# Interleaving the 32x32 products that join the halves of the chunk inverses

## The chip, the cores and the metric

The kernel runs on one core of one Trainium2 chip. Times are microseconds (us) of device time of that core; a kernel's time is the median of its timed runs. The engines are TensorE (PE; its weight loads are PEld), VectorE (DVE), ScalarE (ACT), GpSimd (POOL) and SyncE (SP), which here issues most DMAs.

## What is computed

Two layers of a diffusion trunk over 256 latent and 256 context tokens, width 2048, in float32. Layer 0 is attention; layer 1 is a bidirectional chunked gated DeltaNet with 32 value heads over 16 key heads, chunks of 64 tokens. The change lies in layer 1, in the triangular solve of each chunk:

```python
def gated_delta_chunked(q, k, v, g, beta, state0):
    ...
    kb = kf * bf[..., None]
    lmat = jnp.where(strict, jnp.einsum('bhncd,bhnsd->bhncs', kb, kf) * decay, 0.0)
    rhs = jnp.concatenate([vf * bf[..., None], kb * jnp.exp(gf)[..., None]], axis=-1)
    sol = lax.linalg.triangular_solve(lmat + jnp.eye(CHUNK, dtype=F32), rhs, left_side=True, lower=True)
    u, w = sol[..., :dv], sol[..., dv:]
    ...

def deltanet_layer(x, ctx, c, c_ctx, ...):
    ...
    o_cf, s_cf = gated_delta_chunked(qc, kc, vc, gc[0], bc[0], zero)
    o_xf, _ = gated_delta_chunked(qx, kx, vx, gx[0], bx[0], s_cf)
    o_cb, s_cb = gated_delta_chunked(flip_t(qc), flip_t(kc), flip_t(vc), flip_t(gc[1]), flip_t(bc[1]), zero)
    o_xb, _ = gated_delta_chunked(flip_t(qx), flip_t(kx), flip_t(vx), flip_t(gx[1]), flip_t(bx[1]), s_cb)
    x = x + gt[:, None] * deltanet_out(o_xf + flip_t(o_xb), zx, o_norm, w_out)
```

## The kernel before

Dense products take a weight tile of 128x1024 that SP loads (`raw`, four buffers), ScalarE rounds to `whi` (L77, three buffers) and VectorE subtracts to give the rest `wlo` (L78, three buffers). Each 128x128 block is then used in three matmuls, L90 to L92, over 512 or 256 tokens into a tile `mm` of PSUM. So every weight tile passes through SP, ScalarE, VectorE and TensorE in that order.

Layer 1 first works on keys, queries and decays of 16 heads: `head(kh)` (L672) runs the dense products, the convolution's taps on VectorE (L561), silu on ScalarE (L572, L575), transposes `ptk` (L679), squares (L682) and norms (L701 on GpSimd, L703), decays `pd` (L711 to L716) in PSUM tiles of the tag `xu`, and products `kk` (L727), and stores its results. From two heads `inverse(sg)` (L743) makes the 32 chunk inverses (two heads, two directions, eight chunks), 64x64 each. The two 32x32 diagonal blocks of all of them are inverted at once on VectorE, with 31 steps of two instructions (L768, L770); X is then scaled (L772) and transposed into `U` both ways (L775, L776).

The block between the two halves is what the change touches. For a direction d and a chunk h of a pair, `left(d, h)` (L782) makes 16 products of 32x32 into `px`, which ScalarE evicts, negated, to `Xs` (L789); `right(d, h, Xs)` (L792) makes 16 more into `pu`, which ScalarE copies into `U` (L799). `px` and `pu` are tiles of one bank of PSUM, of the tag `xu` with two buffers. `quad(b, h)` (L588) is the 32 partitions from 64 b + 32 h on; `tile_position` names the 32 rows and 32 columns of TensorE's array that a product uses. In `left` these are rows 32 h and columns 64 + 32 h; in `right`, rows 64 + 32 h, and columns 32 h for d = 0 and 64 + 32 h for d = 1. All 16 products of one call use the same place. The four `left` calls run one ahead of the four `right` calls (L801 to L809), then SP stores `U` (L811). `U`, `X` and `L` have one buffer each. A product in float32 appears in the trace as two matmul records, each with its weight load.

The order is set by generators. The loop at L884 to L893 has 42 rounds, six for one of the inverses 0 to 6; a round takes seven steps of `inverse` (to the next `yield`), in some rounds a step of the gate units `zunits` at the fourth, and then a step of `heads` (`woven`, L832). The joining falls into the sixth round. Inverse 7 runs by itself, with the last gate units and the first values filled in after every fourth step (L897). Then the scans over the chunks begin, with the value heads' dense products between them. The instruction order on each engine is fixed when the program is built, from the order written and from estimated durations.

Of the kernel before, what the change touches and what calls it, by code (L numbers as in the profile page):

```python
# [26 lines left out]
def trunk_kernel(ctx: ExitStack, tc: tile.TileContext, g):  # L27
# [40 lines left out]
    # ---------------------------------------------------------------- helpers  # L68
# [26 lines left out]
    def sliced(wsrc, units, k0, n, xh, xl, pst, first, last):  # L95
        # n contraction tiles of two units
        m = 128 * n
        raw = wp.tile([128, 1024], F32, name="raw", tag="raw", bufs=4)
        for e in range(2):
            nc.sync.dma_start(raw[:, m * e:m * e + m], wsrc[units[e]][:, 128 * k0:128 * k0 + m])  # L100
        w = split(raw, 2 * m)
        for e in range(2):
            dense(pst[e], [w], m * e, n, xh, xl, k0=k0, first=first, last=last)
# [3 lines left out]
    def adaln(l, ps, pm, tp, order, bufs=3, after=None):  # L107
        # a step for every two weight tiles
        wm, bmod, gain = ((g["ab_wm"], ab_bmod, ab_gain), (g["dn_wm"], dn_bmod, dn_gain))[l]
        for f0, n in order:  # L110
            # n blocks of 128 outputs from f0 on
# [35 lines left out]
    def adaln_lanes(l, ps, pm, tp, chunks, after=None):  # L147
        # the sums over the contraction tiles on the vector engine, those over the partitions at the end
# [36 lines left out]
    def rstd_bcast(squares, nb, dim, ps, tag, tp, sq_tag="sq"):  # L185
        # squares: for every block of tokens the tiles that add up to its squares, summed over the feature tiles
# [18 lines left out]
    def add_squares(acc, srcs, first, tp, n=T, sq_tag="sq", last=False):  # L205
        # the last squares stay apart
        sq = acc if first else tp.tile([128, T], F32, name="sq", tag=sq_tag)
        m = n // len(srcs)
        for i, x in enumerate(srcs):
            A.activation(sq[:, i * m:(i + 1) * m], x, AF.Square)  # L210
        if not first and not last:
            V.tensor_tensor(acc[:, :n], acc[:, :n], sq[:, :n], op=ALU.add)
        return sq
# [22 lines left out]
    # ================================================================ layer 0  # L236
# [6 lines left out]
    with tc.tile_pool(name="s0", bufs=2) as tp, tc.tile_pool(name="s0p", bufs=1, space=PSUM) as ps:  # L243
# [6 lines left out]
        # squares, four feature tiles at a time  # L250
# [51 lines left out]
    with tc.tile_pool(name="ab", bufs=2, reuse_waits="tile") as tp, \  # L302
# [29 lines left out]
        def parts(src, name, n=T, scale=1.0, pool=None, bufs=1):  # L332
            # float32 as the sum of two float32r
# [16 lines left out]
        def attend(qT, kT, vT, h, bias=None, rope=None):  # L350
            # v to token-major
# [58 lines left out]
        # latent ranks and the shared rope key  # L410
# [98 lines left out]
    # ================================================================ layer 1  # L509
    # Tokens of a sequence go in two tiles of two chunks, (0, 3) and (1, 2); inside a tile the order is  # L510
    # (half of the chunk, chunk of the pair, token), so that a 32-partition quadrant is 2 * half + chunk,
    # while the keys are worked on, and (chunk of the pair, token) in the scans.
# [54 lines left out]
    def tile_act(dst, src, func, halves):  # L567
        # to tile order, as (half, chunk, token) or (chunk, token)
# [9 lines left out]
    def by_pair(dst, src):  # L578
        # columns from (half, chunk, token) to (chunk, half, token)
        A.copy(dst.rearrange("p s (h b i) -> p s b h i", h=2, b=2), src.rearrange("p s (b h i) -> p s b h i", b=2, h=2))  # L580

    def by_chunk(dst, src):
        # rows from (half, chunk, token) to (chunk, token)
# [22 lines left out]
    def project(u, p):  # L606
        # output unit to the residual, back from tile order
# [5 lines left out]
    # the scans take over the room of the keys' tiles tag by tag, so that they begin as it is left  # L613
    with tc.tile_pool(name="dn", bufs=2, reuse_waits="tile") as tp, \
            tc.tile_pool(name="dnps", bufs=2, space=PSUM, reuse_waits="tile") as ps:
        # write strength and decay of all heads
# [3 lines left out]
        # of the keys: squared norms inverted, and norms, as the rows lie here and in the scans; of the queries, what  # L620
        # stands for the norm's epsilon once they are not normalized
# [35 lines left out]
        for d in range(2):  # L657
# [3 lines left out]
            # scan arrangement a: chunk h of a pair runs in direction (a + h) % 2  # L661
# [10 lines left out]
        def head(kh):  # L672
# [31 lines left out]
            # the decays [row, column]: forwards for the transposed system, backwards for the system  # L704
            # itself and, within the sequence, transposed
# [27 lines left out]
            for d in range(2):  # L733
                # of a 32-block only what lies on its side of the diagonal is read
# [8 lines left out]
        def inverse(sg):  # L743
            # (norm^2 / beta + L)^-1 of two heads, their keys not normalized, L the system forwards and its transpose backwards: of the
            # 32-blocks on the vector engine, with the unit on the partition
            NTu = NTs[sg].rearrange("p a k s h i -> p (a k s h) i")
            # as the blocks come and transposed
# [31 lines left out]
            # the block between the two halves of a chunk  # L779
            lo, hi = slice(0, 32), slice(32, 64)  # L780

            def left(d, h):  # L782
                r1, r2 = quad(0, h), quad(1, h)
                px = ps.tile([128, 16, 32], F32, name="px", tag="xu")
                for u in range(16):
                    PE.matmul(px[r2, u], NTu[r1, 16 * d + u, hi], U[r1, 1, 16 * d + u, lo], start=True, stop=True,
                              tile_position=(r1.start, r2.start))
                Xs = tp.tile([128, 16, 32], F32, name="Xs", tag="Xs")
                A.mul(Xs[r2], px[r2], -1.0)  # L789
                return Xs  # L790

            def right(d, h, Xs):  # L792
                r2 = quad(1, h)
                out, off = (quad(0, h), hi) if d == 0 else (r2, lo)
                pu = ps.tile([128, 16, 32], F32, name="pu", tag="xu")
                for u in range(16):
                    ab = Xs[r2, u], U[r2, 0, 16 * d + u, hi]
                    PE.matmul(pu[out, u], ab[d], ab[1 - d], start=True, stop=True, tile_position=(r2.start, out.start))  # L798
                A.copy(U[out, d, 16 * d:16 * d + 16, off], pu[out])  # L799

            cur = None  # L801
            for d in range(2):
                for h in range(2):
                    nxt = d, h, left(d, h)
                    if cur:
                        right(*cur)
                        yield
                    cur = nxt
            right(*cur)  # L809
# [12 lines left out]
        def mix(main, filler, n):  # L822
            # one step of the filler after every n of the main work
# [8 lines left out]
        def woven():  # L832
            # the heads one after the other, each with its products begun while the one before it ends
# [71 lines left out]
        def cut(t, i, shape):  # L905
            # piece i of a tile, in a shape
# [11 lines left out]
        # block-diagonal operands: the zeros stay, the blocks come from memory  # L918
# [14 lines left out]
        # of keys and values, the parts that the state's products take  # L933
# [6 lines left out]
        def blocks(dst, src):  # L940
            # [128, 2 (direction), 4, 64] in memory to [128, 2 (arrangement), 4, 128]
# [25 lines left out]
        def step(o, n):  # L967
            # one chunk in both directions, in four parts
# [68 lines left out]
        def finish(o):  # L1037
            # norm and gate of a head, in four parts
# [26 lines left out]
        # of the output products, units below NE take the heads below 12 early  # L1065
        NE = 8
        # weight tiles in the order of their use
# [23 lines left out]
        def tile_mm(p, j, k0, xh, xl, sl, first, last):  # L1091
            # the eight contraction tiles of weight tile j, one at a time
# [12 lines left out]
        def value_unit(q):  # L1105
            # q: unit number after those of head 0; its first step is 2 * q - 2
# [57 lines left out]
        for st in range(-2, 64 + LAG):  # L1164
# [27 lines left out]
            # what follows the products of the unit before  # L1192
# [77 lines left out]
def _layout(inputs):  # L1270
# [5 lines left out]
    def fm(a):  # [tok, feat] -> [128, feat/128, tok]  # L1276
        return np.ascontiguousarray(a.T.reshape(-1, 128, a.shape[0]).transpose(1, 0, 2))

    def units(w, kt=None):  # [K, C] -> [C/128, 128, K/128 * 128]
# [3 lines left out]
    def vec(v):  # [F] -> [128, F/128]  # L1283
        return v.reshape(-1, 128).T
# [24 lines left out]
    # neighbourhood bias, padded outside the window  # L1309
# [10 lines left out]
    # constants of the shapes alone  # L1320
# [10 lines left out]
    # gated delta layer  # L1331
# [45 lines left out]
```

## Time and profile before

| | |
|---|---|
| time, median of 3 runs | 2585.1 us (2583.42 to 2586.82) |
| profiled execution: span from first to last instruction | 2580.0 us |
| mean granted TensorE clock of that execution | 0.985 |
| TensorE, VectorE, ScalarE, GpSimd busy, share of the span | 97%, 72%, 44%, 10% |
| matmul instructions | 16586 |

The page gives one execution. A device time of that execution apart from its span is not given; the median of the three runs lies 5.1 us above the span. Busy shares are averages over stages; a matmul's end is modelled, so a busy TensorE is not TensorE at its peak, and its real pace is the distance between starts. "Idle before" and the arrow behind it say how long an engine stood and what ended that.

### The profile page before, as it was taken

The numbers are of one execution on the slowest core, as the hardware profiler recorded it, in microseconds if no ns is written. First come the engines' busy times: TensorE is split into PE (matmuls) and PEld (weight loads), VectorE is DVE, ScalarE is ACT, GpSimd is POOL, SyncE is SP. The second block draws the span as 40 slices with busy tenths as digits, with TensorE's granted clock in tenths as the row PEclk, the third lists the DMA queues.
The fourth block names the chain that finished last, engine by engine and source line by source line (L and its number), as shares of the span: only waits on it lengthen the run. The fifth ranks groups of instructions, "written<-read, shape, count | busy, mean of one in ns | idle before, by whom it ended". The sixth has DMA issues, their size and how long they took to land.

```text
span 2580.0 us, 43446 instructions
## 1 busy us (share of the span) xinstructions
PE 2499.2 (97%) x16586; PEld 2039.0 (79%) x16586; DVE 1852.2 (72%) x3543; ACT 1146.6 (44%) x2484; POOL 267.4 (10%) x261
## 2 busy tenths in 40 slices
PE   6999999999999999989999999999999999999998
PEld 4657888888767788768888889897777777777898
DVE  4544788773455687758999999987677777777754
ACT  4223323232333422377656655643444445445353
POOL 0000000000000000133212222310000000003000
PEclk9999999999999999999999999999999999999999
DMA  8872655532343376644454544563333433335454
GB/s 258 289 247 90 201 172 167 175 114 96 117 153 100 120 230 221 212 139 157 142 156 152 160 138 150 159 213 100 88 99 115 119 99 106 113 91 174 153 188 140
DMA packets 201810, 394.30 MB, mean 153 GB/s; under 512 B 68225, under 2 KB 109697, under 8 KB 201473
## 3 DMA queue, kind: packets, MB, share of 16 engines
q1 hardware_dynamic: 200448, 389.98, 47.9%
q8 instruction: 131, 2.15, 0.4%
q10 hardware_dynamic: 1152, 1.54, 0.2%
q14 instruction: 79, 0.64, 0.1%
HBM read 356.28 MB, written 35.13 MB: 152 GB/s over the span
## 4 chain that ended last, share of the span: by engine, by line
PE 79%; DVE 9%; issue 6%; DMA 3%; ACT 2%; SPq 0%; POOL 0%; DVEq 0%; POOLq 0%; ACTq 0%
PE mm L90 19%; PE mm L91 18%; PE mm L92 18%; PE pks L982 3%; PE pmod L127 3%; DVE wlo L78 2%; PE sp L348 2%; PE ptr L994 2%; DVE X L770 1%; DVE outer L768 1%; PE po L348 1%; PE pu L798 1%; DVE acc L561 1%; PE ptr L1027 1%; PE psu L1013 1%
## 5 line engine op out<-in xcount | busy, mean ns | idle before, releaser
L90 PE MATMUL mm<-hh,whi 128*128 128x512 f32 (+1 forms) x2784 | 988.5, 355 | 3.7 <-ACT t L636 2.2
L92 PE MATMUL mm<-hh,wlo 128*128 128x512 f32 (+1 forms) x2784 | 962.2, 346 | 8.7 <-DVE wlo L78 7.5
L91 PE MATMUL mm<-hl,whi 128*128 128x512 f32 (+1 forms) x2784 | 963.2, 346 | 0.0
L77 ACT CAST whi<-raw 128x1024 fp32r<-128x1024 f32 (+2 forms) x346 | 338.3, 979 | 668.4 <-PE mm L91 515.6
L90 PEld LDWEIGHTS mm<-hh,whi 128*128 128x128 f32 x2784 | 535.7, 192 | 113.8 <-issue 32.6
L92 PEld LDWEIGHTS mm<-hh,wlo 128*128 128x128 f32 x2784 | 535.4, 192 | 73.1 <-DVE wlo L78 9.4
L91 PEld LDWEIGHTS mm<-hl,whi 128*128 128x128 f32 x2784 | 536.0, 193 | 62.2 <-issue 8.4
L78 DVE TENSOR_TENSOR wlo<-raw,whi 128x1024 fp32r<-128x1024 f32 (+2 forms) x346 | 402.7, 1166 | 212.9 <-ACT whi L77 206.1
L163 DVE SCALAR_TENSOR_TENSOR lacc<-mraw,cond,lacc 128x512 f32<-128x512 f32 x300 | 208.8, 749 | 0.0
L561 DVE SCALAR_TENSOR_TENSOR acc<-cin,taps,acc 128x508 f32<-128x508 f32 (+3 forms) x256 | 196.1, 767 | 6.7 <-ACT acc L552 4.3
L1004 DVE SCALAR_TENSOR_TENSOR vl<-ptr,egm,vh 128x128 fp32r<-128x128 f32 x224 | 64.6, 346 | 98.3 <-ACT rf L1001 39.4
L711 POOL TENSOR_TENSOR rhs<-ghl,incl 128x512 fp32r<-128x512 f32 (+1 forms) x96 | 108.4, 1139 | 133.4 <-PE pd L713 114.2
L127 PE MATMUL pmod<-mraw,cond 128*32 128x512 f32 (+2 forms) x640 | 94.3, 501 | 23.2 <-DMA mraw<-ab_wm 18.6
L768 DVE SCALAR_TENSOR_TENSOR outer<-L,bv,X 128x31 f32<-128x31 f32 (+15 forms) x248 | 112.4, 453 | 4.7
L1088 DVE TENSOR_TENSOR wlo<-raw,whi 128x1024 fp32r<-128x1024 f32 x84 | 102.6, 1222 | 14.4 <-ACT whi L1080 13.8
L194 POOL TENSOR_TENSOR rs<-ms,half 128x4 f32<-128x4 f32 (+1 forms) x5 | 4.7, 947 | 985.1 <-DVE ms L192 985.1
L770 DVE TENSOR_TENSOR X<-X,outer 128x31 f32<-128x31 f32 (+15 forms) x248 | 101.7, 410 | 4.6
L575 ACT ACTIVATE ac<-acc 128x128 f32<-128x128 f32 x160 | 37.4, 300 | 146.0 <-DVE acc L561 146.0
L90 PE MATMUL mm<-gh,whi 128*128 128x512 f32 x256 | 99.9, 392 | 1.7 <-DVE x1B L493 1.7
L91 PE MATMUL mm<-gl,whi 128*128 128x512 f32 x256 | 99.9, 390 | 0.2 <-DVE gl L481 0.2
L92 PE MATMUL mm<-gh,wlo 128*128 128x512 f32 x256 | 99.7, 390 | 0.0
L998 ACT ACTIVATE vh<-ptr,egm 128x128 fp32r<-128x128 f32 x224 | 71.0, 373 | 56.6 <-PE ptr L994 54.6
(289 smaller groups left out, 3629.2 us busy)
## 6 DMA issues: line engine op xcount, KB each, us to landing
raw<-dn_w SPq DMA_DIRECT2D x194, 512.0 KB, 4.0
mraw<-dn_wm SPq DMA_DIRECT2D x96, 512.0 KB, 4.7
mraw<-ab_wm SPq DMA_DIRECT2D x88, 512.0 KB, 5.4
raw<-ab_w SPq DMA_DIRECT2D x66, 512.0 KB, 3.8
raw<-dn_wo SPq DMA_DIRECT2D x64, 512.0 KB, 3.7
raw<-ab_wo SPq DMA_DIRECT2D x32, 512.0 KB, 4.6
raw<-ab_w SPq DMA_DIRECT2D x32, 256.0 KB, 3.6
spt<-sp SPq DMA_DIRECT2D x64, 128.0 KB, 2.8
```

The lines of the kernel that those rows point to most:

```text
L77: A.copy(hi[:, :m], raw[:, :m])
L78: V.tensor_tensor(lo[:, :m], raw[:, :m], hi[:, :m].bitcast(F32), op=ALU.subtract)
L90: PE.matmul(ps, wh[:, c], xh[:, k0 + k, sl], start=first and k == 0, stop=False)
L91: PE.matmul(ps, wh[:, c], xl[:, k0 + k, sl], start=False, stop=False)
L92: end = PE.matmul(ps, wl[:, c], xh[:, k0 + k, sl], start=False, stop=last and k == kt - 1)
L127: PE.matmul(pmod[32 * q:32 * q + 32, :m], cond[:, 4 * kg + q, :], raw[c // 1024][:, half + c % 1024:half + c % 1024 + m], start=kg == 0, s ...
L163: V.scalar_tensor_tensor(acc[:, s], raw[:, q], cond[:, k, s:s + 1], acc[:, s], op0=ALU.mult, op1=ALU.add)
L561: V.scalar_tensor_tensor(o3[:, :, i0:i1], p3[:, :, i0 + d:i1 + d], taps[:, ch, t:t + 1], o3[:, :, i0:i1], op0=ALU.mult, op1=ALU.add)
L711: P.tensor_tensor(rhs, ghl[i].bitcast(F32)[:, d, kh * 8:kh * 8 + 2 * n].unsqueeze(2).broadcast_to(sh), incl[:, c].unsqueeze(1).broadcast_t ...
L768: V.scalar_tensor_tensor(o, L[:, rows, k:k + 1].broadcast_to([128, n, m]), bv[:, k:k + 1], X[:, k:k + 1, cols].broadcast_to([128, n, m]), ...
L770: V.tensor_tensor(X[:, rows, cols], X[:, rows, cols], o, op=ALU.subtract)
L1088: V.tensor_tensor(w, raws[j], h.bitcast(F32), op=ALU.subtract)
```

## The change

`left` now takes a direction and makes the products of both chunks, in turn, into one `px` tile; one eviction of 64 partitions follows. The products of `right` of both directions and both chunks run in one loop, four places of the array in turn, into two `pu` tiles; two copies of 64 partitions follow. The `yield`s lie after each `left` and after the copies, three as before. The arithmetic is the same. Comments are also taken out of the file; those lines of the diff are left out here.

```diff
-            def left(d, h):
-                r1, r2 = quad(0, h), quad(1, h)
+            def left(d):
                 px = ps.tile([128, 16, 32], F32, name="px", tag="xu")
                 for u in range(16):
-                    PE.matmul(px[r2, u], NTu[r1, 16 * d + u, hi], U[r1, 1, 16 * d + u, lo], start=True, stop=True,
-                              tile_position=(r1.start, r2.start))
+                    for h in range(2):
+                        r1, r2 = quad(0, h), quad(1, h)
+                        PE.matmul(px[r2, u], NTu[r1, 16 * d + u, hi], U[r1, 1, 16 * d + u, lo], start=True, stop=True,
+                                  tile_position=(r1.start, r2.start))
                 Xs = tp.tile([128, 16, 32], F32, name="Xs", tag="Xs")
-                A.mul(Xs[r2], px[r2], -1.0)
+                A.mul(Xs[64:128], px[64:128], -1.0)
                 return Xs
 
-            def right(d, h, Xs):
-                r2 = quad(1, h)
-                out, off = (quad(0, h), hi) if d == 0 else (r2, lo)
-                pu = ps.tile([128, 16, 32], F32, name="pu", tag="xu")
-                for u in range(16):
-                    ab = Xs[r2, u], U[r2, 0, 16 * d + u, hi]
-                    PE.matmul(pu[out, u], ab[d], ab[1 - d], start=True, stop=True, tile_position=(r2.start, out.start))
-                A.copy(U[out, d, 16 * d:16 * d + 16, off], pu[out])
-
-            cur = None
+            Xs = []
             for d in range(2):
-                for h in range(2):
-                    nxt = d, h, left(d, h)
-                    if cur:
-                        right(*cur)
-                        yield
-                    cur = nxt
-            right(*cur)
+                Xs.append(left(d))
+                yield
+            pu = [ps.tile([128, 16, 32], F32, name="pu", tag="xu") for _ in range(2)]
+            for u in range(16):
+                for d in range(2):
+                    for h in range(2):
+                        r2 = quad(1, h)
+                        out = quad(0, h) if d == 0 else r2
+                        ab = Xs[d][r2, u], U[r2, 0, 16 * d + u, hi]
+                        PE.matmul(pu[d][out, u], ab[d], ab[1 - d], start=True, stop=True,
+                                  tile_position=(r2.start, out.start))
+            for d in range(2):
+                out, off = (slice(0, 64), hi) if d == 0 else (slice(64, 128), lo)
+                A.copy(U[out, d, 16 * d:16 * d + 16, off], pu[d][out])
+            yield
             for d in range(2):
                 by_chunk(spu[sg][:, d], U[:, d, 16 * d:16 * d + 16])
```

## Rows read from the trace of the kernel before

**Rows 1.** The page: busy time of each engine (us, share of the span, instructions), and the chain of work that ended last, by engine.
```profile
PE 2499.2 (97%) x16586; PEld 2039.0 (79%) x16586; DVE 1852.2 (72%) x3543; ACT 1146.6 (44%) x2484; POOL 267.4 (10%) x261
...
PE 79%; DVE 9%; issue 6%; DMA 3%; ACT 2%; SPq 0%; POOL 0%; DVEq 0%; POOLq 0%; ACTq 0%
```

**Rows 2.** Busy time by stretches of the layer-1 stage, in turn the 24 us from the first `px` product of an inverse on and the stretch up to the next one. Columns: stretch, its length, then busy us of PE, PEld, DVE, ACT and POOL with their instructions, mean granted TensorE clock, share of the DMA engines, GB/s.
```profile
1259.00:1283.00 24.00, 23.82 (x401) 22.51 (x401) 21.66 (x44) 14.69 (x32) 4.67 (x8) 1.00 0.52 146
1283.00:1337.00 54.00, 50.89 (x330) 45.87 (x331) 50.15 (x77) 31.94 (x59) 14.76 (x14) 0.94 0.49 156
1337.50:1361.50 24.00, 24.00 (x397) 22.59 (x397) 22.35 (x46) 16.25 (x34) 4.22 (x7) 1.00 0.51 144
1361.50:1413.00 51.50, 49.43 (x375) 44.09 (x375) 50.45 (x74) 30.39 (x58) 14.71 (x16) 0.97 0.47 149
1413.00:1437.00 24.00, 23.45 (x349) 21.87 (x349) 21.18 (x42) 14.55 (x30) 6.83 (x10) 1.00 0.52 160
1437.00:1490.00 53.00, 50.35 (x386) 45.50 (x385) 50.62 (x77) 31.51 (x60) 12.61 (x11) 0.97 0.49 152
1490.00:1514.00 24.00, 23.60 (x339) 22.03 (x338) 20.44 (x43) 13.70 (x29) 6.12 (x9) 0.93 0.52 166
1514.00:1566.60 52.60, 49.31 (x317) 44.09 (x317) 48.33 (x76) 29.25 (x58) 13.96 (x13) 0.94 0.45 141
1566.60:1590.60 24.00, 24.00 (x405) 22.89 (x405) 22.23 (x44) 16.72 (x35) 4.12 (x7) 1.00 0.52 149
1590.60:1641.00 50.40, 46.70 (x296) 41.60 (x295) 48.51 (x73) 30.57 (x57) 16.89 (x15) 0.93 0.49 155
1641.00:1665.00 24.00, 24.00 (x403) 22.54 (x402) 21.77 (x40) 14.49 (x32) 6.20 (x9) 1.00 0.61 160
1665.00:1715.00 50.00, 47.84 (x426) 46.63 (x425) 48.62 (x74) 30.26 (x47) 10.19 (x10) 1.00 0.68 217
1715.00:1739.00 24.00, 21.62 (x317) 19.49 (x314) 17.91 (x33) 8.23 (x15) 2.96 (x4) 0.93 0.62 182
```

**Rows 3.** The instructions that write or read `px` and `pu`, matmuls alone: records, duration of one (ns, least, median, most), starts of the first and the last (us).
```profile
L786 PE MATMUL px<-U,NT x1024: 190/191/258, 1259.0 to 1784.8; 32*32 32x32 f32 x171
...
L798 PE MATMUL pu<-U,Xs x512: 190/191/255, 1265.5 to 1778.2; 32*32 32x32 f32 x171
...
L798 PE MATMUL pu<-Xs,U x512: 191/191/212, 1275.5 to 1789.7; 32*32 32x32 f32 x171
```

**Rows 4.** TensorE's timeline in the first tail: start (us), time from the first start to the last modelled end of the merged records (us), records, and in brackets the idle time before them. The dense products in between are left out but for the one that follows the first `px` records.
```profile
1258.97 2.11 PE L786 MATMUL px<-U,NT 32*32 32x32 f32 x64 [1.31 <-DVE U L776]
1261.01 0.39 PE L92 MATMUL mm<-hh,wlo 128*128 128x256 f32 x1
...
1265.47 1.10 PE L798 MATMUL pu<-U,Xs 32*32 32x32 f32 x29
1266.38 0.21 PE L786 MATMUL px<-U,NT 32*32 32x32 f32 x1
1266.41 0.19 PE L798 MATMUL pu<-U,Xs 32*32 32x32 f32 x1
1266.44 0.19 PE L786 MATMUL px<-U,NT 32*32 32x32 f32 x1
1266.44 0.19 PE L798 MATMUL pu<-U,Xs 32*32 32x32 f32 x1
1266.47 0.19 PE L786 MATMUL px<-U,NT 32*32 32x32 f32 x1
1266.47 0.19 PE L798 MATMUL pu<-U,Xs 32*32 32x32 f32 x1
1266.50 1.08 PE L786 MATMUL px<-U,NT 32*32 32x32 f32 x29
```

**Rows 5.** TensorE's timeline further on: the products `kk`, whose four column groups of 32 take turns, and the dense product that follows.
```profile
1272.54 0.64 PE L727 MATMUL kk<-sp 128*32 128x128 f32 x22
1273.11 0.38 PE L90 MATMUL mm<-hh,whi 128*128 128x256 f32 x1
```

**Rows 6.** ScalarE's timeline in the first tail: a copy of 128 partitions from PSUM, the eviction of the second `px`, a cast of weights, and the first copy into `U`.
```profile
1258.19 0.58 ACT L551 COPY cin<-mm 128x512 f32<-128x512 f32 x1
...
1261.12 0.59 ACT L789 ACTIVATE Xs<-px 32x512 f32<-32x512 f32 x1 [0.33 <-PE px L786]
1263.82 1.05 ACT L77 CAST whi<-raw 128x1024 fp32r<-128x1024 f32 x1 [2.11 <-PE mm L91]
1266.70 0.57 ACT L799 COPY U<-pu 32x512 f32<-32x512 f32 x1 [1.83 <-PE pu L798]
```

**Rows 7.** Who waited for whom, TensorE from 1200 to 1764 us: in total (us), times, longest.
```profile
PE ptk L679 <- ACT ac L572: 14.0, 6, 3.7
```

**Rows 8.** The same of VectorE.
```profile
DVE wlo L78 <- ACT whi L77: 14.6, 13, 2.5
DVE km L703 <- POOL nrm L701: 5.3, 6, 1.6
```

**Rows 9.** Busy time by stretches from the eighth inverse's first product on, and in the scans; columns as in rows 2.
```profile
1770.50:1774.20 3.70, 3.70 (x124) 3.66 (x124) 3.67 (x3) 1.43 (x3) 0.00 (x0) 1.00 0.51 110
1774.20:1784.40 10.20, 8.87 (x77) 6.89 (x74) 4.69 (x7) 5.71 (x14) 0.73 (x1) 0.50 0.38 105
1784.40:1791.00 6.60, 6.60 (x104) 5.48 (x102) 0.61 (x2) 2.10 (x5) 1.85 (x2) 1.00 0.32 79
...
1800.00:1900.00 100.00, 100.00 (x596) 76.58 (x598) 68.41 (x172) 46.79 (x138) 5.40 (x6) 1.00 0.33 96
```

## Prediction

> **What bounds the kernel now.** I read the page first for what is busy, then stretches of the layer-1 stage for which engine still has idle time, then the order of instructions around one inverse, then who waited for whom. The page's busy shares do not say where this change acts: TensorE is busy 97% of the span and most of the chain that ended last is TensorE [rows 1], but those are averages over stages. The lines touched (L786, L789, L798, L799) run only from 1259 to 1790 us. There seven inverses are woven into the heads' products, one about every 76 us, and an eighth stands alone at 1764 to 1791. I call the 24 us from the first `px` product on an inverse's tail.
>
> In the seven tails TensorE is busy 21.6 to 24.0 of 24 us, while VectorE is idle 24 − 21.66 = 2.34, then 1.65, 2.82, 3.56, 1.77, 2.23 and 6.09 us, 20.5 us in all [rows 2]. So TensorE is late there. In the six stretches between tails, 311.5 us, VectorE is busy 296.7, idle 14.8 [rows 2]: there it is VectorE that sets the pace, and TensorE's own idle time there is mostly the transposes `ptk` waiting for ScalarE's silu (14.0 us, six waits [rows 7]), which in turn follows VectorE's taps. The reader should see two engines that take turns, each with about 5% in reserve. Time freed on TensorE counts in the tails only until VectorE is the late one.
>
> **The products.** There are 1024 records of `px` and twice 512 of `pu`, with a weight load each [rows 3], so 2048 over eight inverses, 256 in each; a product in the code is two records. In the first tail 64 `px` records take from 1258.97 to 1261.01, where the next work starts: 2.04 us, 31.9 ns a record [rows 4]. One inverse therefore costs 256 × 31.9 ns = 8.17 us of TensorE, all eight 65.3 us. All 32 records of a group lie in one quadrant of the array.
>
> The trace of before already shows what neighbours in different quadrants do, at the seam where a `pu` group ends and a `px` group begins: `px` at 1266.38, `pu` .41, `px` .44, `pu` .44, `px` .47, `pu` .47, `px` .50 [rows 4]. Two records start in each 31 ns, and `px` runs ahead although the last `pu` records were issued before it. So the 31 ns is a quadrant's pace, not the queue's. In `left` the two chunks alternate, rows 0 to columns 64 and rows 32 to columns 96: two quadrants, 16 ns a record, 128 × 16 ns = 2.04 us. In `right` four quadrants take turns. The nearest rows are the `kk` products, four column groups in turn: 22 records of 64 to 128 columns start within 1273.11 − 1272.54 = 0.57 us, 26 ns each, less than the 31.9 ns that a record of only 32 columns costs when alone in its quadrant [rows 4, 5]. I take four at a time, 8 ns, 1.02 us for 128; the upper bound is two at a time, 2.04 us. Sum for an inverse: 8.17 − 2.04 − 1.02 = 5.1 us less TensorE time (lower bound 4.1); for eight, 41 us (33).
>
> Those seams join products that write different tiles of PSUM. After the change, both chunks of `left` write one `px` tile, from different row groups of the array; no row shows that, since `kk` has four column groups over all rows. The Trainium skill, TensorEngine Tiling (Array Packing), section Gotcha 1: PSUM Pressure, says that different row tiles cannot access the same PSUM bank at the same time. By that rule the chunks could not overlap, and only the two directions of `right` would, which is a rival below.
>
> **The evictions.** Four `Xs` and four `U` copies of 32 partitions per inverse become two and two of 64. A 32x512 eviction takes 0.59 and 0.57 us and a copy of 128x512 from PSUM 0.58 [rows 6], so partitions cost nothing: 4 × 0.58 = 2.3 us less ScalarE per inverse. ScalarE is busy 14 to 17 of 24 us in the tails [rows 2]. I cost this at zero, hidden by that idle time; if the cover is gone, because a cast `whi` stands behind an eviction that waits, it gives at most those 2.3 us per tail. They are the same microseconds of VectorE idle time that the products free, so they are not added.
>
> **The waits.** `right` now needs both `Xs` and releases nothing until all its 128 records are done, so the first `U` copy comes later relative to its own products, though before the place of the old last copy. Queued behind the first `pu` on TensorE are dense products and the next head's `ptk` and `pd`; `px` and `pu` fill both buffers of the tag `xu`, as now, and the next `pd` waits for one. The second `Xs` is there 0.6 us after the last `px` (1261.12 + 0.59 against 1261.08 [rows 4, 6]); with one cast of 1.05 us in front [rows 6] it is 1.7 us. Between 1261.01 and 1265.47 TensorE does dense products [rows 4], which hide that; without that cover it costs 1.7 us per tail out of the 5.1, 13.6 over eight. I take zero, and keep 1.7. The `spu` stores leave SP behind the last copies and, in the woven inverses, behind one gate unit's weight loads; the next writer of `U` is a memset needed 31 steps later. Zero, with the rest of the period as cover.
>
> **What becomes of 5.1 us.** In the first six tails VectorE's idle time is 14.4 us. The named waits there are the norms from Pool (5.3 us, behind the `ptk` squares) and `wlo` behind ScalarE's cast [rows 8]. Part of it is TensorE's lateness, part a chain through Pool that stays. I take half, 7.2 us (ends 0 and 14.4). In the seventh tail 6.1 us are idle and the wait is on casts that wait for TensorE; I take 4 (0 to 5.1). Between tails the lead that TensorE keeps can remove some of the 14.8 us; as VectorE sets the pace I take a quarter, 3.7 (0 to 10).
>
> The eighth inverse is different. VectorE is idle there (0.61 busy of 6.60 us, then 68 of 100) and TensorE goes on busy without a break into the scans [rows 9]. Here the whole 5.1 us should pass. Also, the 3.7 us from 1770.5 on hold 124 records, almost nothing but 32-column products, one at a time, and the granted clock then stands at 0.50, the 1.2 GHz level, for 10.2 us [rows 9]. What half the clock costs there is up to 5.1 us. With the products done in fewer microseconds the stretch holds more dense work, but a later fall is as possible; I take half, 2.5 (0 to 5.1).
>
> Sum: 7.2 + 4 + 3.7 + 5.1 + 2.5 = 22.5 us. The profiled execution's span is 2580.0 us, 2557.5 after. The three runs have their median at 2585.1, 5.1 us above that span, which I leave as it is: 2562.6, say 2563 us. What is late next in the woven stage is VectorE.
>
> **The rivals.**
> VectorE takes over at once: its idle time in and between tails is latency through Pool and ScalarE, and TensorE's new lead turns into standing at `ptk`. For it: VectorE is busy 147.5 + 296.7 of 168 + 311.5 us in these stretches, 93% [rows 2], and the waits of rows 8 that name no TensorE work. Against it: the idle time is denser in the tails. Only the eighth inverse gains, 5.1 + 2.5: 2577 us.
>
> Overlap is halved: two chunks on one PSUM tile do not run together. `left` stays at 4.08 us, `right` at two quadrants 2.04 us, so 2.04 us are saved per inverse. With the shares above (half in tails 6 us, eighth 2 us): 2577 us. The Trainium skill's rule quoted above would give this. Speaking against it: four `kk` column groups already write one tile together [rows 5]; the row groups are what is unshown.
>
> All of it passes: TensorE's 41 us are taken everywhere, VectorE's idle time of 20.5 + 14.8 allowing nearly that: 2585 − 40 = 2545 us.
>
> Slower: the freed time becomes standing at `ptk`, and the standing costs clock. The stretches between tails, where TensorE waits for `ptk` (up to 3.7 us at once [rows 7]), have in five of six a mean granted clock of 0.93 to 0.97 (0.94 over 54 us is 54 × 0.06 × 2 = 6.5 us at half speed), while five of seven tails have 1.00 [rows 2]. If each of six periods gets one more such fall of 6.8 us, and TensorE does dense work that VectorE needs next, 3.4 us are lost in each: 20.4, less the 7.6 of the eighth inverse, 2585 + 13 = 2598 us. It decides once a fall costs more than VectorE's lead at that place, about 2.5 us. Against it: TensorE then has 5 us in reserve per period to pay with.
>
> **How the numbers follow.** Forecast 0.52 (2553 to 2573, its terms not all at one end), VectorE at once 0.14, half the overlap 0.13, all passes 0.08, slower 0.13. Faster by over 0.2% (5.2 us, about what a measurement of this kernel can tell from no change) takes the forecast, all-passes and just over half of the two at 2577: 0.75. Within: the weaker half of those and a little of the slower case, 0.14. Slower: 0.11. For 8 in 10 the range goes from the all-passes case to no change: 2545 to 2586, leaving out the slower case and the fringes.
>
> **What would show it.** Right: `px` records start two in 31 ns and `pu` four; a tail's products take about 3 us instead of 8; the evictions stay at 0.58 us and halve in number; VectorE's idle time in the tails falls from 20.5 us to about 9; the eighth inverse ends some 5 us sooner and the clock's 10.2 us at half shrink. Wrong: `px` at 31 ns a record (the PSUM tile binds), VectorE idle as before with TensorE standing at `ptk` (VectorE took over), or mean clock between tails under 0.93 (the slower case).

## The result, and the profile after

The changed kernel takes 2569.0 us (2568.78 to 2569.72, four runs) against 2584.6 us (2583.42 to 2586.82, four runs beside it): ratio 0.9945, 95% interval 0.9931 to 0.9959, 15.6 us faster. The profiled executions differ by 13.0 us of span, 2580.0 to 2567.0; rows below account for those 13.0. The page of the kernel after, engines and chain, answers to [rows 1]:

```profile
PE 2464.1 (96%) x16586; PEld 2004.8 (78%) x16586; DVE 1849.9 (72%) x3543; ACT 1126.9 (44%) x2452; POOL 271.2 (11%) x261
...
PE 75%; DVE 12%; issue 6%; DMA 3%; ACT 3%; SPq 0%; POOL 0%; DVEq 0%; POOLq 0%; ACTq 0%
```

The number of matmuls is the same and TensorE is busy 35 us less; ScalarE has 32 instructions fewer; VectorE's share of the chain that ended last has grown from 9% to 12%, TensorE's fallen from 79% to 75%.

TensorE's timeline in the first tail after (start, time to the last modelled end, records; rows of `pu` between its first and last are left out), to be read beside [rows 4]:

```profile
1260.46 2.21 PE L788 MATMUL px<-U,NT 32*32 32x32 f32 x128 [1.31 <-DVE U L776]
1262.60 0.39 PE L92 MATMUL mm<-hh,wlo 128*128 128x256 f32 x1
...
1265.66 0.22 PE L805 MATMUL pu<-U,Xs 32*32 32x32 f32 x2
...
1266.76 0.21 PE L805 MATMUL pu<-Xs,U 32*32 32x32 f32 x2
...
1271.57 0.69 PE L679 MATMUL ptk<-ident,ac 128*128 128x128 f32 x2 [4.60 <-ACT ac L572]
```

128 `px` records now take 2.14 us, as 64 did before, and 128 `pu` records start within 1.12 us, 8.7 ns each: 3.3 us of products instead of 8.2. After them TensorE stands for 4.6 us.

ScalarE in the same tail, to [rows 6]: one eviction of 64 partitions lasts as long as one of 32 did.

```profile
1261.71 0.59 ACT L791 ACTIVATE Xs<-px 64x512 f32<-64x512 f32 x1 [0.86 <-PE px L788]
...
1272.14 1.19 ACT L809 COPY U<-pu 64x512 f32<-64x512 f32 x2
```

The stretches of the stage after, cut at each inverse's first `px` product as in [rows 2], with the same columns:

```profile
1260.50:1284.50 24.00, 19.40 (x387) 18.60 (x388) 21.28 (x39) 11.14 (x25) 7.66 (x10) 0.86 0.46 133
1284.50:1338.70 54.20, 50.66 (x347) 45.22 (x345) 51.16 (x83) 33.57 (x62) 12.99 (x11) 1.00 0.51 161
1338.70:1362.70 24.00, 19.11 (x384) 18.32 (x385) 21.35 (x38) 12.26 (x27) 7.56 (x10) 0.86 0.45 133
1362.70:1413.00 50.30, 46.57 (x319) 41.52 (x317) 48.46 (x79) 32.70 (x60) 12.76 (x12) 1.00 0.49 155
1413.00:1437.00 24.00, 22.29 (x405) 21.34 (x406) 23.48 (x37) 13.01 (x29) 10.04 (x12) 0.86 0.50 149
1437.00:1488.50 51.50, 47.49 (x328) 42.66 (x326) 49.63 (x84) 30.45 (x58) 9.79 (x9) 1.00 0.52 164
1488.50:1512.50 24.00, 23.59 (x414) 22.39 (x415) 23.11 (x36) 13.49 (x29) 10.23 (x12) 0.86 0.47 144
1512.50:1564.00 51.50, 47.70 (x304) 42.61 (x304) 47.64 (x83) 25.38 (x53) 10.91 (x9) 0.93 0.49 154
1564.00:1588.00 24.00, 21.12 (x417) 19.66 (x416) 23.62 (x39) 15.54 (x32) 9.39 (x12) 1.00 0.46 134
1588.00:1638.30 50.30, 45.94 (x310) 40.54 (x308) 48.65 (x82) 28.30 (x55) 12.03 (x10) 1.00 0.53 162
1638.30:1662.30 24.00, 23.74 (x410) 22.07 (x411) 22.73 (x39) 13.04 (x29) 10.28 (x13) 0.86 0.59 162
1662.30:1712.40 50.10, 48.87 (x423) 47.74 (x422) 47.28 (x75) 31.96 (x50) 6.64 (x5) 1.00 0.75 237
1712.40:1736.40 24.00, 21.73 (x327) 17.80 (x328) 22.07 (x41) 6.85 (x11) 3.91 (x6) 0.93 0.72 183
```

Three things are to be seen. VectorE's idle time in the seven tails is 2.72, 2.65, 0.52, 0.89, 0.38, 1.27 and 1.93 us, 10.4 in all, where it was 20.5. Between the tails it is 3.04 + 1.84 + 1.87 + 3.86 + 1.65 + 2.82 = 15.1 us, where it was 14.8: nothing was gained there. And the half clock has moved. Before, five of seven tails ran at 1.00 and five of the six stretches between at 0.93 to 0.97; now five of seven tails have 0.86 (24 × 0.14 × 2 = 6.7 us at half speed) and five of the six stretches between have 1.00. In sum the time at 0.50 from 1200 us to the first products of the scans has grown from 44 to 58 us, which is worth at most half the difference, some 7 us.

The clock falls behind a stand. In the first tail TensorE does nothing from the last `pu` on, and the next stretch has half the clock:

```profile
1266.90:1270.50 3.60, 0.07 (x8) 0.00 (x0) 3.60 (x9) 0.00 (x0) 0.00 (x0) 1.00 0.81 230
1270.50:1277.30 6.80, 5.73 (x26) 5.71 (x27) 5.16 (x12) 3.28 (x13) 0.00 (x0) 0.50 0.57 185
```

The time that the products gave up has partly become such stands: from 1200 to 1760 us TensorE waits 21.1 us for silu before `ptk` (14.0 before [rows 7]) and 8.2 us for VectorE's transposes before `px`.

```profile
PE ptk L679 <- ACT ac L572: 21.1, 10, 4.9
PE px L788 <- DVE U L776: 8.2, 6, 2.5
```

The eighth inverse, to [rows 9]:

```profile
1762.89 3.46 PE L788 MATMUL px<-U,NT 32*32 32x32 f32 x122 [4.69 <-DVE U L776]
```

```profile
1757.90:1762.90 5.00, 0.31 (x4) 0.04 (x3) 4.93 (x4) 0.00 (x0) 0.00 (x0) 0.91 0.00 0
1762.90:1775.60 12.70, 11.24 (x270) 10.14 (x271) 6.87 (x7) 6.71 (x15) 2.51 (x3) 0.50 0.55 136
```

Of the 206 records of dense products that lay between the seventh and the eighth inverse before, 46 now lie ahead of the seventh. TensorE has run out of dense work and stands 4.69 us until VectorE has transposed X; then all joining products, and the first steps of the scans, run at half the clock.

Where the 13.0 us of span lie, from the first starts of `px` and of the scans' products in both traces: the first inverse begins 1.5 us later (1259.0 to 1260.5); first to eighth inverse takes 502.4 us instead of 511.6, 9.1 less, over the same 2509 records of dense products; eighth to the scans' first product 13.1 instead of 15.3, 2.2 less; from there to the end 790.9 instead of 794.1, 3.2 less. −1.5 + 9.1 + 2.2 + 3.2 = 13.0. (First to seventh is 3.5 us shorter, 451.9 instead of 455.4, and seventh to eighth 5.6, 50.5 instead of 56.1, but because of the 46 records these two hold different work and can't be compared one by one.)

The stretch from the first to the eighth inverse shows how much of TensorE's gain counts. Before and after, columns as in [rows 2]:

```profile
1258.97:1770.54 511.57, 491.07 (x4857) 447.79 (x4858) 473.80 (x784) 293.65 (x564) 119.28 (x129) 0.97 0.50 155
1260.46:1762.89 502.43, 460.05 (x4858) 418.30 (x4859) 474.21 (x786) 275.97 (x536) 124.17 (x129) 0.95 0.52 157
```

TensorE is busy 31.0 us less and stands 21.9 us longer (20.5 before, 42.4 after). VectorE is busy as long as before, and its idle time has fallen by 9.6 us (37.8 to 28.2), about as much as the stretch has become shorter.

### The profile page after: what moved, and what is told of

Its sections match the earlier page's. It is cut to its first block, busy times and chain, and to the rows that moved or that the text cites. A ratio compares the mean times of both kernels' runs of the same rounds, so it can differ in the third digit from the quotient of the medians.

```text
span 2567.0 us, 43390 instructions
## 1 busy us (share of the span) xinstructions
PE 2464.1 (96%) x16586; PEld 2004.8 (78%) x16586; DVE 1849.9 (72%) x3543; ACT 1126.9 (44%) x2452; POOL 271.2 (11%) x261
## 4 chain that ended last, share of the span: by engine, by line
PE 75%; DVE 12%; issue 6%; DMA 3%; ACT 3%; SPq 0%; POOL 0%; DVEq 0%; POOLq 0%; ACTq 0%
PE mm L90 19%; PE mm L91 17%; PE mm L92 17%; PE pks L983 3%; PE pmod L127 3%; DVE wlo L78 3%; PE sp L348 2%; PE ptr L995 2%; DVE acc L561 2%; DVE outer L768 1%; PE po L348 1%; DVE X L770 1%; DVE U L776 1%; PE ptr L1028 1%; DMA mraw<-dn_wm 1%
## 5 line engine op out<-in xcount | busy, mean ns | idle before, releaser
L78 DVE TENSOR_TENSOR wlo<-raw,whi 128x1024 fp32r<-128x1024 f32 (+2 forms) x346 | 401.8, 1163 | 210.5 <-ACT whi L77 209.1
L768 DVE SCALAR_TENSOR_TENSOR outer<-L,bv,X 128x31 f32<-128x31 f32 (+15 forms) x248 | 118.2, 476 | 5.2
L770 DVE TENSOR_TENSOR X<-X,outer 128x31 f32<-128x31 f32 (+15 forms) x248 | 99.4, 401 | 4.7
```

What stands on the lines that cost most here:

```text
L78: V.tensor_tensor(lo[:, :m], raw[:, :m], hi[:, :m].bitcast(F32), op=ALU.subtract)
L768: V.scalar_tensor_tensor(o, L[:, rows, k:k + 1].broadcast_to([128, n, m]), bv[:, k:k + 1], X[:, k:k + 1, cols].broadcast_to([128, n, m]), ...
L770: V.tensor_tensor(X[:, rows, cols], X[:, rows, cols], o, op=ALU.subtract)
```

## The experiments

Theory 1: the gain is TensorE time in the tails, and VectorE takes over before all of it counts. Theory 2: the gain is ScalarE's fewer evictions. Theory 3: it is the order in which the build lays the other instructions, which changes with any edit. Ratios are to the kernel before on the same chip; below 1 is faster.

**Merged evictions, products in sequence.** The loops are nested the other way:

```diff
-                for u in range(16):
-                    for h in range(2):
+                for h in range(2):
+                    for u in range(16):
...
-            for u in range(16):
-                for d in range(2):
-                    for h in range(2):
+            for d in range(2):
+                for h in range(2):
+                    for u in range(16):
```

> One px tile per direction, one eviction of 64 partitions and one pu loop at the end, as after the change, but the products are written chunk by chunk and direction by direction, so that neighbours share a quadrant. Theory 1 (the gain is TensorE time in the tails): records at 31 ns again, 8.2 us of products per inverse, time within 3 us of before, 2582 to 2588 us. Theory 2 (the gain is ScalarE's fewer evictions and waits): about 2569 us, as after the change. Theory 3 (the gain comes from the new order in which the build lays the other instructions): about 2569 us too, since no other variant has an order on the engines so near to the changed kernel's.

Measured: 2596.5 us, ratio 1.0048 (1.0031 to 1.0066), slower than before. So half the evictions gain nothing by themselves, and theory 2 is out as the main cause. Theory 3 is out too: the dense products lie among the inverses almost as in the changed kernel (2351 records from the first to the seventh and 158 to the eighth, against 2349 and 160), and only the order of the small products differs. That it is slower than the kernel before goes beyond all three. From 1200 to 1764 us its products take 31.5 + 32.2 us, as before (31.6 + 31.5), but they come in two pieces, all of `px` and later all of `pu`, with no dense work between chunks. Its first tail, TensorE's timeline and then stretches:

```profile
1261.72 4.32 PE L788 MATMUL px<-U,NT 32*32 32x32 f32 x128 [1.31 <-DVE U L776]
```

```profile
1261.70:1265.00 3.30, 3.27 (x112) 3.28 (x113) 3.30 (x2) 1.01 (x2) 0.00 (x0) 1.00 0.55 122
1265.00:1271.80 6.80, 6.80 (x53) 6.51 (x51) 6.70 (x16) 1.53 (x2) 1.11 (x2) 0.50 0.51 149
```

TensorE is busy without a gap with products in one quadrant at a time, and the granted clock still halves, as before the change in the eighth inverse [rows 9]. The stand of 1.31 us just ahead is in the changed kernel too, and there the clock stayed at 1.00 until 1270.5 us. Over the 564 us the mean granted clock is 0.93 against 0.97 before, 0.04 × 564 = 23 us of full-speed work lost. That accounts for more than the 12 us; that it is the cause is argued from these rows, not isolated.

**Products in turn, evictions in quarters.**

```diff
-                A.mul(Xs[64:128], px[64:128], -1.0)
+                for h in range(2):
+                    A.mul(Xs[quad(1, h)], px[quad(1, h)], -1.0)
...
-                out, off = (slice(0, 64), hi) if d == 0 else (slice(64, 128), lo)
-                A.copy(U[out, d, 16 * d:16 * d + 16, off], pu[d][out])
+                for h in range(2):
+                    out, off = (quad(0, h), hi) if d == 0 else (quad(1, h), lo)
+                    A.copy(U[out, d, 16 * d:16 * d + 16, off], pu[d][out])
```

> Products alternate as after the change, but px and pu are evicted in quarters of 32 partitions, eight evictions per inverse as before. Theory 1: products about 3.1 us per inverse, 2566 to 2573 us. Theory 2: within 3 us of before, 2582 to 2588 us. Theory 3: no definite value.

Measured: 2573.1 us, 0.9958 (0.9942 to 0.9974). The whole gain, within the intervals, comes with eight evictions as before. Theory 2 falls.

**`left` alone, `right` alone.** In the first variant, `right` runs by direction and chunk, each with its own `pu` and copy; in the second, `left` runs by chunk, each with its own `px` and eviction:

```diff
+            for d in range(2):
+                for h in range(2):
+                    ...
+                    pu = ps.tile([128, 16, 32], F32, name="pu", tag="xu")
+                    for u in range(16):
+                        ...
+                    A.copy(U[out, d, 16 * d:16 * d + 16, off], pu[out])
```

```diff
+                for h in range(2):
+                    r1, r2 = quad(0, h), quad(1, h)
+                    px = ps.tile([128, 16, 32], F32, name="px", tag="xu")
+                    for u in range(16):
+                        ...
+                    A.mul(Xs[r2], px[r2], -1.0)
```

> left as after the change, right by chunk and direction with its own pu tile and a 32-partition copy each. Products 2.04 + 4.1 = 6.1 us per inverse instead of 8.2 or 3.1. Theory 1, with time in proportion: 2585 - 15.6 * 2.0 / 5.0 = 2578 us. Theory 1 with VectorE as the limit that cuts the gain off early: nearer to after, 2570 to 2575 us. Theory 2 (six evictions): about 2581 us.

> right as after the change, left chunk by chunk with a px tile and a 32-partition eviction each: products 4.1 + 1.1 = 5.2 us per inverse instead of 8.2 or 3.1. Theory 1 with VectorE as the cap: 2570 to 2575 us, like left alone. If the two halves of the change simply add, and left alone gave 0.36%, right alone gives about 0.2%: 2578 to 2581 us.

Measured: `left` alone 2573.5 us, 0.9964 (0.9952 to 0.9977); `right` alone 2570.0 us, 0.9959 (0.9944 to 0.9975). The changed kernel again beside the second:

> The changed kernel again, beside these: a ratio of 0.993 to 0.996 to the kernel before, so that the differences among the variants can be read on one chip.

Measured: 2570.2 us, 0.9952 (0.9940 to 0.9965). The halves don't add: 0.36% and 0.41% make 0.77%, both together give 0.48% to 0.55%. The first 2 to 3 us of TensorE time per inverse buy most of what 4.9 us buy. This agrees with theory 1 with an early cap, but the clock differs as well: its mean from 1200 to 1764 us is 0.98 with `left` alone, 0.97 with `right` alone and 0.96 with both, so these three do not tell a cap by VectorE from one by the clock.

**Every product made twice.** `[*range(16)] * 2` in place of `range(16)` in both loops.

> As after the change, with every px and pu product made twice: 6.2 us of products per inverse. In proportion to TensorE time: about 2578 us. With VectorE as the limit that already cut the gain off: 2570 to 2574 us, because the first microseconds taken back are TensorE's idle time. Theory 2: about 2569 us.

Measured: 2630.0 us, 1.0181 (1.0165 to 1.0197), outside every theory. It is no clean dose of TensorE time: who waited for whom, TensorE from 1200 to 1830 us:

```profile
PE mm L92 <- DVE wlo L78: 14.6, 5, 6.5
PE pu L805 <- issue: 14.5, 11, 2.4
...
PE px L788 <- issue: 6.1, 5, 1.5
```

In the midst of the products TensorE stands 20.6 us for nothing that the profile shows, which the single set does not do, and the mean granted clock from 1200 to 1764 us is 0.89 against 0.96. The run says that a doubled run of such products costs much more than twice its time, without showing why, and nothing on the cap.

**VectorE lightened, before and after.** The two instructions of every second step are left out in the seven woven inverses:

```diff
             for k in range(31):
+                if sg < 7 and k % 2:
+                    yield
+                    continue
```

> The kernel before, with the two VectorE instructions of every second of the 31 steps left out in the seven woven inverses (those inverses are then not the reference's): about 13 us less VectorE work per inverse. If VectorE takes over from TensorE once the products are fast, this shows nothing by itself but the base: about 2545 to 2565 us, TensorE the late engine all through the woven stage.

> The changed kernel with the same VectorE steps left out. Theory 1 with VectorE as the cap: with VectorE out of the way the freed TensorE time counts nearly whole, so this is 25 to 40 us below the lightened kernel before, against 15.6 us between the unlightened two. Rival (the gain is cut off by waits or by TensorE's granted clock, not by VectorE's work): the difference stays at 10 to 20 us.

Measured: before, lightened, 2585.5 us, 1.0014 (1.0005 to 1.0024); after, lightened, 2553.7 us, 0.9895 (0.9877 to 0.9913). Busy time from 1200 to 1764 us of the two, before first:

```profile
1200.00:1764.00 564.00, 530.20 (x5247) 484.94 (x5246) 456.17 (x665) 330.01 (x627) 139.07 (x141) 0.96 0.51 157
```

```profile
1200.00:1764.00 564.00, 525.11 (x5564) 475.74 (x5564) 467.77 (x683) 326.96 (x638) 141.46 (x145) 0.96 0.53 163
```

VectorE is busy 456 and 468 us, where unlightened it is 524 and 533. Before the change that buys nothing, and the 2545 to 2565 us expected of it were missed. The run doesn't say that TensorE alone was late: TensorE's waiting has moved, from 14.0 to 2.6 us for silu at `ptk` and from 7.5 to 31.2 us for `wlo`, which in turn waits 81.7 us for ScalarE's `whi`. After the change the lightening buys 0.50% more than the change alone, and the change itself is then worth 0.0119 × 2581 = 31 us instead of 15.6, of 39 us of TensorE time.

These two kernels have the dense products at the same places among the inverses, so that they can be compared stretch by stretch. From the first to the eighth inverse, before first:

```profile
1242.90:1762.20 519.30, 489.89 (x4892) 448.09 (x4884) 416.87 (x610) 301.35 (x568) 127.61 (x129) 0.96 0.51 156
1243.10:1734.80 491.70, 458.28 (x4893) 418.14 (x4884) 415.62 (x609) 284.36 (x539) 126.00 (x129) 0.95 0.54 165
```

TensorE is busy 31.6 us less, and 27.6 of them count; with VectorE's full work it was 9.1 of 31.0. So VectorE's work keeps some 15 to 19 us of the change's TensorE time from counting. A part of that goes through the clock: the change adds 14 us at 0.50 to the full kernels and 3 us to the lightened ones, worth 7 and 2 us at most. In both lightened kernels TensorE waits long for `wlo` (31.2 and 27.1 us, against 7.5 and 7.8 in the unlightened), so the 31 us is what this pair shows, not a law.

**Dense filler ahead of `px`,** to hold the clock: 

```diff
+                if d == 0:
+                    for _ in range(20 if sg == 7 else 10):
+                        PE.matmul(px.rearrange("p u j -> p (u j)"), seg[:, 0], hh[:, 0, :], start=True, stop=True)
```

> The changed kernel with dense products whose results are overwritten (10, in the eighth inverse 20, of 128 rows and 512 columns) into px ahead of its first products, where TensorE stands for VectorE's transposes (4.7 us in the eighth inverse, some 1.3 to 2.5 in others) and its clock falls to half behind. Theory (the fall of the clock takes back a part of the gain): half-clock time around the tails shrinks and the time is 2 to 8 us below the changed kernel's, although TensorE does some 20 us more. Rival (the clock only falls where TensorE has time to spare): same time as the changed kernel or up to 6 us more.

Measured: 2579.9 us, 0.9991 (0.9980 to 1.0002), about 12 us slower than the changed kernel for 90 × 0.227 = 20 us of filler. The build laid the first ten at 1245.08 us, 15 us ahead of the stand they were meant for, and the mean clock from 1200 to 1764 us stayed at 0.96. In the eighth inverse the twenty lie right ahead of `px`, from 1764.5 to 1769.0 us, and there the clock held: over the `px` and `pu` products, where the changed kernel has 0.50, the stretch reads

```profile
1770.60:1779.00 8.40, 8.40 (x278) 7.12 (x278) 4.99 (x6) 3.38 (x11) 1.86 (x2) 1.00 0.53 136
```

So filler at its place can hold the clock, but as a whole it does not pay, and what the falls of the clock cost is not settled by it.

**The transposes that the joining needs, first.** `for b, t in ((0, 1), (1, 0), (0, 0), (1, 1))`, with t the second index of `U`.

> The changed kernel with VectorE's four transposes into U in another order: first the one that left needs, then the one that right needs. left can begin 2 us sooner after X is done, with no more work on any engine. Theory that TensorE's standing at px, and the clock behind it, is what is left in the tails: 3 to 10 us below the changed kernel. Rival (VectorE's total work is the cap, so when px starts makes no difference but in the eighth inverse): 0 to 3 us below.

Measured: 2573.4 us, 0.9966 (0.9954 to 0.9977): no gain. With the eighth inverse counted, TensorE stands 7.9 us at `px` (12.9 in the changed kernel) and 28.8 at `ptk` (21.1). An earlier `px` only moves the stand.

**VectorE lightened with no work left out,** as a version that might beat both: every sixth or fourth `wlo` of the woven stage on GpSimd.

```diff
+        e = P if woven_on[0] % 6 == 0 else V
-        V.tensor_tensor(lo[:, :m], raw[:, :m], hi[:, :m].bitcast(F32), op=ALU.subtract)
+        e.tensor_tensor(lo[:, :m], raw[:, :m], hi[:, :m].bitcast(F32), op=ALU.subtract)
```

> The changed kernel with every sixth of the wlo subtractions of the woven stage on GpSimd instead of VectorE: some 19 of 1.2 us each, 23 us less VectorE work and the same results. Theory (after the change VectorE's work is the cap of the woven stage; lightening it by 91 us gave some 13 us): 4 to 13 us below the changed kernel. Rival (a wlo on GpSimd takes about 1.9 us, queues behind the decays' chain there, and TensorE waits for it): no gain or up to 10 us slower.

> The same with every fourth, some 29, 35 us less VectorE work. Theory: as e9 or up to 4 us better. Rival: worse than e9 by the longer queue on GpSimd.

Measured: 2584.2 us, 1.0007 (0.9995 to 1.0018), and 2598.0 us, 1.0061 (1.0049 to 1.0073). The gain of the change is gone. The groups by line from 1200 to 1764 us with every sixth (busy us, mean ns of one, idle before; L774, L776 and L84 are L768, L770 and L78 of the other kernels):

```profile
L774 DVE SCALAR_TENSOR_TENSOR outer<-L,bv,X 128x175 f32<-128x175 f32 (+15 forms) x241 | 128.5, 533 | 5.6
L84 DVE TENSOR_TENSOR wlo<-raw,whi 128x1024 fp32r<-128x1024 f32 x98 | 122.9, 1257 | 18.5 <-ACT whi L79 18.4
...
L776 DVE TENSOR_TENSOR X<-X,outer 128x175 f32<-128x175 f32 (+15 forms) x241 | 112.0, 465 | 5.2
...
L84 POOL TENSOR_TENSOR wlo<-raw,whi 128x1024 fp32r<-128x1024 f32 x17 | 44.8, 2635 | 54.3 <-ACT whi L79 44.7 <-DMA spk<-sp 6.3 <-issue 3.1
```

and in the changed kernel:

```profile
L768 DVE SCALAR_TENSOR_TENSOR outer<-L,bv,X 128x192 f32<-128x192 f32 (+15 forms) x241 | 114.9, 477 | 5.0
L770 DVE TENSOR_TENSOR X<-X,outer 128x192 f32<-128x192 f32 (+15 forms) x241 | 96.3, 400 | 4.6
```

A `wlo` takes 2.6 us on GpSimd, not 1.9, and the steps on VectorE take 533 and 465 ns on average instead of 477 and 400. The timeline shows how. A step that begins just after a `wlo` on GpSimd lasts about until that ends:

```profile
1351.54 2.39 POOL L84 TENSOR_TENSOR wlo<-raw,whi 128x1024 fp32r<-128x1024 f32 x1 [0.86 <-ACT whi L79]
1351.65 2.48 DVE L774 SCALAR_TENSOR_TENSOR outer<-L,bv,X 128x175 f32<-128x175 f32 x1
```

Beside the 17 `wlo` on GpSimd 21 such steps run; 13 of them take 2.0 to 2.6 us where the same step takes 0.2 to 0.5 with GpSimd idle, the other eight take their usual time. That adds 27 us, more than the 17 × 1.26 = 21 us that were moved away: VectorE is busy 533.6 us of the 564, as against 533.4, and nothing was freed. The Trainium skill, SBUF — State Buffer, section Who interferes with whom, says that a VectorE instruction with two inputs from SBUF contends with a GpSimd instruction that reads SBUF; the rows agree. TensorE waits longer too (13.2 us for `wlo` instead of 7.8, 25.6 at `ptk` instead of 21.1), and the mean clock is 0.93 instead of 0.96; how much of the lost time each of these makes, the run does not separate.

None of the variants that does all the work is reliably faster than the changed kernel.

## Why the prediction was right, step by step

The direction and the mechanism held, and the time lies in the range; the forecast of 22.5 us was 6.9 too large against the medians, and 9.5 against the spans, by which the terms below are measured.

**Products, held.** 2.04 + 1.02 us were forecast and 2.14 + 1.12 measured, 4.9 us saved per inverse where 5.1 were expected. The rival from the Trainium skill (TensorEngine Tiling (Array Packing), Gotcha 1: PSUM Pressure), by which two row groups could not write one bank at once, is refuted in this form: here they write different partitions of it, and 128 records take the time of 64.

**Evictions at zero, held.** 0.59 us for 64 partitions; the two runs that separate evictions from order show no gain from them.

**Waits at zero, held in the first tail, not in the eighth inverse.** In the first tail `pu` starts at 1265.66, 2.3 us after the second `Xs` has ended (ScalarE's second eviction started at 1262.72 and took 0.59). In the eighth inverse there is no dense work to cover it, and the 1.7 us kept aside came nearly whole. From 1200 to 1830 us:

```profile
PE pu L805 <- ACT Xs L791: 1.5, 1, 1.5
```

**VectorE's idle time in the tails, held.** 20.5 − 7.2 − 4 = 9.3 us forecast, 10.4 measured, and the idle time that went did count: from the first to the eighth inverse VectorE is idle 9.6 us less and the stretch is 9.1 us shorter. With the lead between tails the forecast for this stretch was 7.2 + 4 + 3.7 = 14.9.

**The lead between tails, failed.** 3.7 us were forecast; VectorE's idle time there went from 14.8 to 15.1 us. The lead became stands at `ptk` and `px` (29.3 us of both after, against 14.0 and 1.7 before). The sentence that VectorE sets the pace between tails is not borne out for the kernel before, where lightening it gained nothing; for the changed kernel, where it gained 0.50% (13 us), it is.

**The eighth inverse, mis-sized.** 5.1 + 2.5 us were forecast, 2.2 came. The prediction assumed that TensorE still had dense work up to `px`, as before; with its lead, and 46 dense records moved ahead of the seventh inverse, it had none, stood 4.69 us, and the clock stood at 0.50 for the 12.7 us that followed, longer than the 10.2 of [rows 9]. That is the slower rival's mechanism, at one place and at a smaller price.

**Not forecast:** the 1.5 us by which the first inverse starts later, and the 3.2 us gained in the scans, where no line was edited. The runs don't settle their cause; without the two the sum is 9.1 + 2.2 = 11.3 us, so 1.7 of the 13.0 are luck. As an edit can give a new instruction order, I read differences among the variants below 0.2% as nothing.

**VectorE takes over at once,** the rival, holds for more than half of the time: of 39 us of TensorE time 15.6 counted, and 31 with VectorE lightened.

## What to carry to other kernels

Small products that sit in one part of TensorE's array should take turns with neighbours in other parts: two in turn halved their time and four in turn nearly quartered it, with evictions that cost no more for twice the partitions. Before counting the gain, find how much idle time the next engine has in the same stretches: that, 20.5 us here and not the 39 us freed, was the better estimate. And give each engine that gets a lead something to do with it, since here TensorE, where it ran out of work, lost clock for what came next.

## What was not expected of the hardware

- Records in another quadrant start ahead of up to three records that are earlier in the order written (in the kernel before, 1266.38 us on [rows 4]), and two row groups write one PSUM tile side by side: 16.7 ns a `px` record (2.14 us for 128), 8.7 ns a `pu` record, 31.9 ns alone.
- A TensorE that is busy without a gap can still lose its clock: after 3.3 us of 32-column products in one quadrant at a time, 3.27 us of them busy, 6.8 us at 0.50 followed (merged evictions, products in sequence).
- With every product made twice (512 records in each inverse, each with its load) TensorE stood 20.6 us in all, over eight inverses, for nothing that the profile shows.
- A subtraction on GpSimd can hold a VectorE step for its whole length (2.0 to 2.6 us instead of 0.2 to 0.5, 13 of 21 steps beside it). With every sixth `wlo` moved, VectorE's steps became slower by 12% and 16% on average (533 against 477 ns, 465 against 400), which cost more than the move took off.
